# The first gate's vector on TensorE in column groups, and products of the second norm moved into the attention

## The chip, the cores and the metric

The kernel runs on one NeuronCore of a Trainium2 chip. Its engines run side by side, each through its own instruction stream in the order in which the program has it: TensorE (PE, with the weight loads PEld), VectorE (DVE), ScalarE (ACT), GpSimd (POOL), and SyncE (SP), which here issues every DMA. They meet at semaphores. The metric is the device time of one launch in microseconds; it was measured three times for the kernel before, with a median of 1086.33 us (1077.45 to 1088.35).

## The reference

One decoder layer, batch 1, 256 tokens, width 2048, everything in fp32. A conditioning vector `c` makes six vectors of 2048 numbers, which scale, shift and gate the two halves of the layer:

```
mod = silu(c) @ w_mod + b_mod                 # (2048) @ (2048, 12288)
sh1, sc1, g1, sh2, sc2, g2 = split(mod, 6)
h = rmsnorm(x, attn_norm_g) * (1 + sc1) + sh1
proj = h @ w_in                               # 2048 -> 1856
mix = concat(sliding window attention (16 heads, 2 kv heads), latent attention (8 heads))
x = x + g1 * (mix @ w_out)
h = rmsnorm(x, mlp_norm_g) * (1 + sc2) + sh2
x = x + g2 * (relu(h @ w_ff1) ** 2 @ w_ff2)   # 2048 -> 8192 -> 2048
out = rmsnorm(x, final_norm_g)
```

Each of the six vectors is a matrix-vector product with 16.8 MB of `w_mod`.

## The kernel before, in words

Activations are kept transposed: 128 features on the partitions, 256 tokens along the free axis, 16 tiles for the width. The stages follow each other.

1. **Input projection** (lines 242 to 268). For each of 16 feature tiles, `mod_col` makes one column of `sc1` and one of `sh1`, the tile is normalized, and 15 fp32 matmuls add it into eight PSUM banks with a tile `wi` of `w_in`.
2. **Attention** (lines 474 to 583). Twelve units of four heads each, eight of the windowed kind and four of the latent kind. In each step of the loop PE turns a unit's probabilities (`turn`, L376), makes the scores of the unit two steps ahead (`scores`, L405, L446, L447), three up-projections (`fill`, L509, L516) and the values (`values`, L422, L461). DVE and ACT do the softmax. All these matmuls are fp32.
3. **Output projection** (lines 608 to 629). Two halves of 16 output tiles. The weights `wo` come in, are split into a high and a low part (ACT L191, DVE L192), and three matmuls of 256 columns each (L197 to L199) are made for each pair of tiles. DVE adds `g1 * result` to `x` (L620).
4. **Second norm and first feed-forward quarter** (lines 625 to 680): the sum of squares, the reciprocal root `r2` on ACT and DVE, the 16 tiles `h2` on POOL, ACT and DVE, and the same three matmuls with `w_ff1a` (tiles `pf`).
5. **The rest of the feed-forward and the last norm**, which the change does not touch.

`mod_col(part, i)` (line 157) makes 128 numbers of one of the six vectors: a DMA of 1 MB (128 rows of the transposed `w_mod`) into a tile `wm`, and one DVE instruction (L167) that multiplies it with the broadcast vector `c_bc` and sums along 2048 elements. 96 of these make the six vectors. Part 2 is `g1`; its 16 are written before the attention, along with the first `NPRE` = 6 of the 32 products of `sc2` and `sh2` (parts 4 and 3). `pump_mod(n)` takes the next n of those 32: the output projection takes 8 in its second half (PB), the first feed-forward quarter the rest, one per tile of `kt` (LEADK), more where a tile needs them.

The written order is not the final one. A scheduler orders each engine's stream by its own estimate; the attention stands under a high priority and goes ahead of what is written before it where it can. Tiles come from rings: `wm` outside stage 1 has a ring of 2 buffers (tag `rawm`), `wi` and the other weights one of 3, the split weights `whi` and `wlo` 3 each, PSUM 8 banks. A DMA that refills a buffer waits on SP for the buffer's last reader, and all later DMAs stand behind it.

Of the kernel before, what the change touches and what calls it, by code (L numbers as in the profile page):

```python
# [9 lines left out]
F32 = mybir.dt.float32  # L10
F32R = mybir.dt.float32r
AF = mybir.ActivationFunctionType
ALU = mybir.AluOpType

P = 128
D = 2048
# [16 lines left out]
NG = 384  # L33
NPRE = 6
EVP = "A"
NORM = 'AVA'
NG1 = 0
NFILL = 3
NM = 2
NW = 3  # L40
PA = (0, 0)
PB = (0, 1)
LEAD = 0
# [6 lines left out]
LEADK = (1, 1)  # L50
PBN = 8


@with_exitstack
def kernel(
# [4 lines left out]
    vecs: bass.AP,  # L60
    w_mod: bass.AP,
    w_in: bass.AP,
    sinks: bass.AP,
# [93 lines left out]
    def mod_col(part, i):  # L157

        t = (early_ring if part < 2 else lambda n: ring("m", n))(f"wm{part}_{i}")
        nc.sync.dma_start(t, w_mod[part * KT + i])  # L160
        col = small(f"mod{part}_{i}")
# [62 lines left out]
    nc.sync.dma_start(sk_sb, sinks.broadcast_to([P, 16]))  # L224
    nsk_sb = at.tile([P, 16], F32, name="nsk_sb")
    V.tensor_scalar(out=nsk_sb, in0=sk_sb, scalar1=-1.0, scalar2=None, op0=ALU.mult)
# [57 lines left out]
    nc.sync.dma_start(con, consts)  # L284
    g1 = []
    bias_t = actp.tile([P, 16, S], F32, tag="a1", name="bias")
# [6 lines left out]
    mix = [actp.tile([P, 8, 2 * S], F32R, tag="a0", name="mix0")]  # L293
    for d in range(NG1):
        g1.append(mod_col(2, d))
    wukv = raw("wukv")
# [12 lines left out]

    for d in range(NG1, KT):  # L310
        g1.append(mod_col(2, d))
    pump_mod(NPRE)

# [159 lines left out]
    with tc.high_priority():  # L473
# [95 lines left out]
        for n, u in enumerate(units):  # L569
            if n == 8:  # L570
                mix.append(actp.tile([P, 8, 2 * S], F32R, tag="a1", name="mix1"))
            u.turn()
            if n + 2 < len(units):
                units[n + 2].scores()
            if n + 1 < len(units):
                units[n + 1].rows()
            fill(NFILL)
            u.values()


# [24 lines left out]
    for half in range(2):  # L605
# [4 lines left out]
        for dp in range(8):  # L610
            w = raw(f"wo{half}_{dp}")
            nc.sync.dma_start(w, w_out[half, dp])
            for d2 in range(2):
# [8 lines left out]
                if half:  # L622
                    ss2.add(d)
                if half == 0 or dp < PBN:
                    pump_mod((PA, PB)[half][d2])

# [173 lines left out]
def _pack(inp):  # L800
# [8 lines left out]
    def cols(a):  # L809
# [4 lines left out]
                                   cols(inp["mla_kv_norm_g"])], axis=1))  # L814
    d["w_mod"] = cc(np.asarray(inp["w_mod"])[0].T).reshape(96, P, D)
    ar = np.arange
# [23 lines left out]

_ORDER = ["xT", "cT", "vecs", "w_mod", "w_in", "sinks", "rel", "w_uq", "w_ukv", "w_out", "w_ff1a", "w_ff1b", "w_ff2",
          "consts", "onehot", "gmask"]
# [20 lines left out]
```

## Time and profile before

| | before |
|---|---|
| three runs | 1077.45, 1086.33, 1088.35 us |
| profiled execution: its own time, and its span | 1076.42 us, 1074.6 us |
| PE busy | 1025.7 us (95%), 6068 instructions |
| PE weight loads busy | 893.2 us (83%) |
| DVE busy | 744.3 us (69%), 996 instructions |
| ACT, POOL busy | 493.4 us (46%), 112.0 us (10%) |
| mean granted clock of PE | 0.985 |
| DMA | 278.21 MB, mean 259 GB/s |
| chain that ended last | PE 85%, DVE 5%, POOL 3%, DMA 3%, the rest 4% |

The span runs from the first to the last instruction; the execution's own time holds 1.8 us more. A "busy" share counts from an instruction's start to its end, and the ends of matmuls are modelled, so the pace of matmuls is better read from start to start. The trace records each fp32 matmul as two: two passes over the same columns.

### The profile page before, as it was taken

The numbers are of one execution on the slowest core, as the hardware profiler recorded it, in microseconds if no ns is written. First come the engines' busy times: TensorE is split into PE (matmuls) and PEld (weight loads), VectorE is DVE, ScalarE is ACT, GpSimd is POOL, SyncE is SP. The second block draws the span as 40 slices with busy tenths as digits, with TensorE's granted clock in tenths as the row PEclk, the third lists the DMA queues.
The fourth block names the chain that finished last, engine by engine and source line by source line (L and its number), as shares of the span: only waits on it lengthen the run. The fifth ranks groups of instructions, "written<-read, shape, count | busy, mean of one in ns | idle before, by whom it ended". The sixth has DMA issues, their size and how long they took to land.

```text
span 1074.6 us, 15326 instructions
## 1 busy us (share of the span) xinstructions
PE 1025.7 (95%) x6068; PEld 893.2 (83%) x6068; DVE 744.3 (69%) x996; ACT 493.4 (46%) x836; POOL 112.0 (10%) x88
## 2 busy tenths in 40 slices
PE   5999999999995999999999999999999999999995
PEld 4777756679995999888888888888888888888884
DVE  5777568689996789798775555556555666556564
ACT  2100076553443333784445665333666433465552
POOL 0000003000246545000000000000000000001122
PEclk9899999999998999999999999999999999999997
DMA  8999976689997765788885555555555555555542
GB/s 328 426 426 427 417 291 236 240 298 365 428 424 289 269 244 231 267 336 339 313 312 196 195 181 186 187 192 197 196 187 180 188 192 195 196 190 180 182 155 78
DMA packets 42344, 278.21 MB, mean 259 GB/s; under 512 B 4832, under 2 KB 7456, under 8 KB 11424
## 3 DMA queue, kind: packets, MB, share of 16 engines
q1 hardware_dynamic: 42272, 277.23, 68.1%
q8 instruction: 47, 0.77, 0.3%
q14 instruction: 25, 0.20, 0.1%
HBM read 275.09 MB, written 2.12 MB: 258 GB/s over the span
## 4 chain that ended last, share of the span: by engine, by line
PE 85%; DVE 5%; POOL 3%; DMA 3%; issue 2%; ACT 2%; SPq 1%; DVEq 0%; ACTq 0%; POOLq 0%
PE pd L203 22%; PE pu L203 16%; PE pd L204 11%; PE pj L268 9%; PE pu L204 9%; PE pd L198 2%; PE pd L197 2%; PE pd L199 2%; POOL xn L641 2%; DVE wm L167 2%; PE pf L199 1%; PE pf L197 1%; PE pf L198 1%; DMA wi<-in_w_in 1%; DMA wm<-in_w_mod 1%
## 5 line engine op out<-in xcount | busy, mean ns | idle before, releaser
L192 DVE TENSOR_TENSOR wf_l<-wf,wf_h 128x1024 fp32r<-128x1024 f32 x256 | 313.6, 1227 | 199.0 <-ACT wf_h L191 196.1
L191 ACT ACTIVATE wf_h<-wf 128x1024 fp32r<-128x1024 f32 x256 | 269.9, 1057 | 242.9 <-PE pd L203 177.7
L203 PE MATMUL pd<-u,wf_h 128*128 128x512 f32 x1024 | 357.0, 393 | 0.0
L204 PE MATMUL pd<-u,wf_l 128*128 128x256 f32 x1024 | 286.9, 280 | 0.0
L203 PE MATMUL pu<-h,wf_h 128*128 128x512 f32 x768 | 266.5, 391 | 0.0
L203 PEld LDWEIGHTS pd<-u,wf_h 128*128 128x128 f32 x1024 | 191.7, 187 | 43.3 <-DVE u L655 0.2
L204 PE MATMUL pu<-h,wf_l 128*128 128x256 f32 x768 | 215.1, 280 | 0.0
L204 PEld LDWEIGHTS pd<-u,wf_l 128*128 128x128 f32 x1024 | 193.5, 189 | 0.1
L203 PEld LDWEIGHTS pu<-h,wf_h 128*128 128x128 f32 x768 | 143.6, 187 | 31.4
L167 DVE CUSTOM_DVE_ANT_0 wm<-wm,c_bc,vec 128x2048 f32<-128x2048 f32 x64 | 151.7, 2370 | 1.6 <-DMA wm<-in_w_mod 1.6
L204 PEld LDWEIGHTS pu<-h,wf_l 128*128 128x128 f32 x768 | 145.2, 189 | 0.3 <-DVE wf_l L192 0.3
L268 PE MATMUL pj<-h,wi 128*128 128x256 f32 (+1 forms) x480 | 111.5, 389 | 9.6 <-ACT h L257 9.3
L268 PEld LDWEIGHTS pj<-h,wi 128*128 128x128 f32 (+1 forms) x480 | 88.1, 189 | 32.7 <-issue 11.4
L594 POOL TENSOR_TENSOR sqa<-sqa,sqr 128x256 f32<-128x256 f32 x26 | 31.8, 1222 | 717.6 <-ACT sqr L592 717.6
L167 DVE CUSTOM_DVE_ANT_0 wm<-wm,c_bc,b 128x2048 f32<-128x2048 f32 x32 | 77.3, 2414 | 28.4 <-DMA wm<-in_w_mod 28.4
L197 PE MATMUL pf<-h,wf_h 128*128 128x256 f32 x256 | 73.2, 290 | 8.6 <-ACT h L643 7.2
L199 PE MATMUL pf<-h,wf_l 128*128 128x256 f32 x256 | 72.1, 289 | 4.9 <-DVE wf_l L192 4.9
L198 PE MATMUL pf<-h,wf_h 128*128 128x256 f32 x256 | 73.1, 288 | 0.0
L197 PE MATMUL pd<-mix,wo_h 128*128 128x256 f32 x256 | 72.9, 285 | 0.0
L198 PE MATMUL pd<-mix,wo_h 128*128 128x256 f32 x256 | 72.4, 283 | 0.0
L199 PE MATMUL pd<-mix,wo_l 128*128 128x256 f32 x256 | 72.3, 283 | 0.0
L197 PEld LDWEIGHTS pf<-h,wf_h 128*128 128x128 f32 x256 | 50.2, 197 | 9.4 <-ACT h L643 7.6
(169 smaller groups left out, 1014.0 us busy)
## 6 DMA issues: line engine op xcount, KB each, us to landing
wm<-in_w_mod SPq DMA_DIRECT2D x96, 1024.0 KB, 8.1
wf<-in_w_ff SPq DMA_DIRECT2D x64, 1024.0 KB, 4.8
wf<-in_w_ff1b SPq DMA_DIRECT2D x48, 1024.0 KB, 4.8
wo<-in_w_out SPq DMA_DIRECT2D x16, 1024.0 KB, 10.1
wf<-in_w_ff1a SPq DMA_DIRECT2D x16, 1024.0 KB, 8.4
wi<-in_w_in SPq DMA_DIRECT2D x15, 928.0 KB, 12.2
x_sb<-in_xT SPq DMA_DIRECT2D x4, 512.0 KB, 6.5
bias<-g_dr SPq DMA_DIRECT2D x2, 1024.0 KB, 12.8
```

The costliest lines, as they stand in the source:

```text
L167: V.tensor_tensor_reduce(out=t, in0=t, in1=c_bc, scale=1.0, scalar=init, op0=ALU.mult, op1=ALU.add, accum_out=col)
L191: A.activation(out=hi, in_=src, func=AF.Copy)
L192: V.tensor_tensor(out=lo, in0=src, in1=hi.bitcast(F32), op=ALU.subtract)
L197: T.matmul(out, lhsT=wh, rhs=a[:, 0:S], start=start, stop=False, **kw)
L198: T.matmul(out, lhsT=wh, rhs=a[:, S : 2 * S], start=False, stop=False, **kw)
L199: T.matmul(out, lhsT=wl, rhs=a[:, 0:S], start=False, stop=stop, **kw)
L203: T.matmul(out, lhsT=wh, rhs=a, start=start, stop=False)
L204: T.matmul(out[:, 0:S], lhsT=wl, rhs=a[:, 0:S], start=False, stop=stop)
L268: T.matmul(proj(j)[: e - j * P, :], lhsT=w[:, j * P : e], rhs=h, start=(kt == 0 and j % 2 == 0), stop=(kt == KT - 1), skip_group_check=True)
L594: G.tensor_tensor(out=sqa, in0=sqa, in1=sq, op=ALU.add)
L641: G.tensor_scalar(out=xn, in0=x_sb[:, kt, :], scalar1=a2, scalar2=None, op0=ALU.mult)
```

## The change

`g1` no longer comes from DVE. `w_mod` loses its part 2, and a new input `w_g1` holds that part untransposed (2048 inputs by 2048 outputs). For each of 16 tiles of 128 inputs, `gate_steps` loads 1 MB and makes four matmuls: the stationary operand is the column `ce` of silu(c), broadcast to 32 columns, the moving one 512 outputs of `w_g1`. Matmul q writes PSUM partitions 32q to 32q+31, so the four stand in four different column groups of the array. All 64 add into one bank, `pg1`, which stays taken meanwhile. Even tiles are loaded as two halves into buffers of the rings `whi` and `wlo`, odd ones into `rawm`. `gate_out` copies the bank on ACT, turns it with four transposes, and one DVE instruction adds the bias and picks the 16 columns.

`GSTEPS` gives two tiles to each of the first eight units. `MSTEPS` gives 12 of the products of the second norm to the twelve units (6 stood there before), and `PA`, `PB` give five to each half of the output projection (0 and 8 before). So 22 instead of 14 are written ahead of the first feed-forward quarter, and 10 instead of 18 are left to it. The buffer `nsk_sb` now shares `sk_sb`.

```diff
-NPRE = 6
-NG1 = 0
-PA = (0, 0)
-PB = (0, 1)
-PBN = 8
+GSTEPS = (2, 2, 2, 2, 2, 2, 2, 2, 0, 0, 0, 0)
+MSTEPS = (0, 1, 1, 1, 1, 1, 1, 1, 2, 2, 1, 0)
+PA = (1, 3, 4, 6, 7)
+PB = (0, 1, 3, 5, 6)
...
-    for d in range(NG1, KT):
-        g1.append(mod_col(2, d))
-    pump_mod(NPRE)
+    gate = {"kt": 0, "ps": None}
+    g1_all = small("g1_all", KT)
+    g1 = [g1_all[:, d : d + 1] for d in range(KT)]
+
+    def gate_steps(n):
+        if gate["kt"] == 0:
+            gate["ps"] = bank("pg1")
+        for _ in range(n):
+            kt = gate["kt"]
+            if kt == KT:
+                return
+            if kt % 2:
+                t = ring("m", f"wg{kt}")
+                nc.sync.dma_start(t, w_g1[kt])
+                t = [t[:, 0:1024], t[:, 1024:2048]]
+            else:
+
+                t = [splp.tile([P, 1024], F32, tag=f"w{i}", name=f"wg{kt}{i}") for i in ("hi", "lo")]
+                for i in range(2):
+                    nc.sync.dma_start(t[i], w_g1[kt, :, i * 1024 : (i + 1) * 1024])
+            for q in range(4):
+                T.matmul(gate["ps"][32 * q : 32 * q + 32, :], lhsT=ce[:, kt : kt + 1].broadcast_to([P, 32]),
+                         rhs=t[q // 2][:, 512 * (q % 2) : 512 * (q % 2) + 512], start=(kt == 0),
+                         stop=(kt == KT - 1), skip_group_check=True)
+            gate["kt"] += 1
+
+    def gate_out():
+        rows = at.tile([P, 512], F32, tag="pT", name="g1_rows", bufs=4)
+        A.activation(out=rows, in_=gate["ps"], func=AF.Copy)
+        pt1 = bank("pt1")
+        for j in range(4):
+            T.transpose(out=pt1[:, j * P : (j + 1) * P], in_=rows[:, j * P : (j + 1) * P], identity=ident)
+
+        V.tensor_tensor(out=g1_all.rearrange("p (q j) -> p j q", j=4),
+                        in0=pt1.rearrange("p (j q r) -> p j q r", j=4, q=4)[:, :, :, 0],
+                        in1=vec[:, V_BMOD + 32 : V_BMOD + 48].rearrange("p (q j) -> p j q", j=4), op=ALU.add)
...
             fill(NFILL)
+            gate_steps(GSTEPS[n])
+            pump_mod(MSTEPS[n])
             u.values()
+            if n == 9:
+                gate_out()
...
-                if half == 0 or dp < PBN:
-                    pump_mod((PA, PB)[half][d2])
+                if d2 and dp in (PA, PB)[half]:
+                    pump_mod(1)
```

How it moves the streams, at three places. On PE, in the third unit of the attention (`puqn` and `pukn` are up-projections, `poa` values, `pta` transposes, `pg` the gate's bank, `wg4hi` and `wg4lo` the halves of input tile 4), before:

```order
L509 MATMUL puqn_1050<-cq_781,wuq_lo_189 128x256
L509 MATMUL puqn_1050<-cq_782,wuq_lo_191 128x256
L509 MATMUL pukn_1056<-ckv,wukv 128x256
L422 MATMUL poa_1060<-pTa_1021,vA 64x512
L376 MATMUL pta_1062<-ident,ssa_968 128x128 x4
```

and after:

```order
L540 MATMUL puqn_995<-cq_693,wuq_lo_188 128x256
L540 MATMUL puqn_995<-cq_694,wuq_lo_190 128x256
L540 MATMUL pukn_1001<-ckv,wukv 128x256
L329 MATMUL pg_858<-wg4hi,ce 32x512 x2
L453 MATMUL poa_1023<-pTa_966,vA 64x512
L329 MATMUL pg_858<-wg4lo,ce 32x512 x2
L407 MATMUL pta_1025<-ident,ssa_895 128x128 x4
```

The four matmuls of an input tile stand here as two pairs, with a matmul of the values between them.

On SP, at the end of the input projection (`wi` are the last tiles of `w_in`, `wm_15` the last products of stage 1, `con`, `bias` and `wukv` what the attention needs first), before:

```order
L160 DMA wm_15_635<-in_w_mod 128x2048
L265 DMA wi_645<-in_w_in 128x1856
L265 DMA wi_662<-in_w_in 128x1024
L265 DMA wi_662<-in_w_in 128x832
L284 DMA con<-in_consts 128x896
L289 DMA bias<-g_dr 128x8x256 x2
L297 DMA wukv<-in_w_ukv 128x2048
```

and after:

```order
L160 DMA wm_15_634<-in_w_mod 128x2048
L265 DMA wi_644<-in_w_in 128x1856
L321 DMA wg_867<-in_w_g 128x2048
L321 DMA wg_947<-in_w_g 128x2048
L265 DMA wi_661<-in_w_in 128x1024
L265 DMA wi_661<-in_w_in 128x832
L284 DMA con<-in_consts 128x896
L288 DMA bias<-g_dr 128x8x256 x2
L294 DMA wukv<-in_w_ukv 128x2048
```

Two gate tiles of 1 MB each stand ahead of the last tile of `w_in`; their buffers are those of the two products `wm_15`.

On DVE, at the second norm (`r_a`, `r_y` make the reciprocal root, `xn` and `h` the first tile, `wm` a product, `wf_l` a split weight), before:

```order
L620 SCALAR_TENSOR_TENSOR x_sb<-pd_15_2521,mod_15_754,x_sb 128x256
L179 TENSOR_SCALAR r_a<-pr_2514 128x256
L636 TENSOR_TENSOR a_0_2578<-mod_0_758,vec 128x1
L180 SCALAR_TENSOR_TENSOR r_a<-r_a,r_y 128x256
L181 TENSOR_TENSOR r_a<-r_a,r_y 128x256
L167 ISA wm_7_2706,mod_7_2708<-wm_7_2706,c_bc,vec 128x2048
L167 ISA mod_7_2708 128x1
L182 SCALAR_TENSOR_TENSOR r_y<-r_a,r_y 128x256
L192 TENSOR_TENSOR wf_l_2609<-wf_2572,wf_h_2608 128x1024
L639 SCALAR_TENSOR_TENSOR xn_0_2580<-x_sb,a_0_2578,r_y 128x256
```

and after:

```order
L655 SCALAR_TENSOR_TENSOR x_sb<-pd_15_2614,g_all,x_sb 128x256
L167 ISA wm_11_2795,mod_11_2797<-wm_11_2795,c_bc,vec 128x2048
L167 ISA mod_11_2797 128x1
L179 TENSOR_SCALAR r_a<-pr_2607 128x256
L671 TENSOR_TENSOR a_0_2667<-mod_0_955,vec 128x1
L192 TENSOR_TENSOR wf_l_2698<-wf_2661,wf_h_2697 128x1024
L180 SCALAR_TENSOR_TENSOR r_a<-r_a,r_y 128x256
L192 TENSOR_TENSOR wf_l_2739<-wf_2725,wf_h_2738 128x1024
L181 TENSOR_TENSOR r_a<-r_a,r_y 128x256
L182 SCALAR_TENSOR_TENSOR r_y<-r_a,r_y 128x256
L674 SCALAR_TENSOR_TENSOR xn_0_2669<-x_sb,a_0_2667,r_y 128x256
```

A product still stands at the norm, now ahead of the root instead of inside it, and two splits stand between the root's instructions.

## Rows read from the trace of the kernel before

**Rows 1.** By stage: window, length, busy PE, PEld, DVE, ACT, POOL; clock, DMA share, GB/s

```profile
136.70:230.00 93.30, 88.14 (x406) 58.00 (x406) 72.60 (x184) 63.21 (x195) 12.18 (x15) 1.00 0.68 252
230.00:321.50 91.50, 90.49 (x753) 90.24 (x753) 86.34 (x99) 37.70 (x46) 18.04 (x14) 1.00 0.98 398
321.50:346.00 24.50, 16.25 (x119) 15.53 (x118) 15.70 (x25) 7.99 (x13) 14.57 (x12) 0.86 0.82 315
346.00:460.00 114.00, 107.61 (x811) 103.36 (x810) 95.69 (x105) 55.09 (x89) 44.76 (x19) 0.99 0.68 253
```

**Rows 2.** Three of these stages, DVE on `wm` alone; clock, DMA share, GB/s

```profile
136.70:230.00 93.30, 36.73 (x16) 1.00 0.68 252
230.00:321.50 91.50, 36.84 (x16) 1.00 0.98 398
346.00:460.00 114.00, 41.31 (x17) 0.99 0.68 253
```

**Rows 3.** Waits of PE, 136.7 to 230 us: total, times, longest

```profile
PE pob L461 <- ACT pTb L366: 1.3, 2, 0.7
PE prq L467 <- ACT qr L366: 1.2, 2, 0.7
...
PE pvb L516 <- DVE ckv L322: 0.9, 1, 0.9
```

**Rows 4.** Waits of PE, 230 to 460 us

```profile
PE pf L197 <- ACT h L643: 7.2, 1, 7.2
PE pf L199 <- DVE wf_l L192: 4.9, 4, 3.0
PE pf L197 <- ACT wf_h L191: 1.5, 2, 0.9
```

**Rows 5.** PE's timeline: start, length, line, tiles, array rows*columns, shape, count

```profile
207.45 1.03 PE L509 MATMUL puqn<-cq,wuq_hi 128*128 128x256 f32 x4
208.31 0.59 PE L509 MATMUL puqn<-cq,wuq_lo 128*128 128x256 f32 x2
...
216.58 0.70 PE L446 MATMUL scb<-kn,qn 128*128 128x256 f32 x2
217.21 0.70 PE L447 MATMUL scb<-kra,qr 64*128 64x256 f32 x2
```

**Rows 6.** PE's timeline where two tilings of 64 rows meet

```profile
144.79 0.45 PE L562 MATMUL prk_a<-kr,seli 64*128 64x256 f32 x1 [0.65 <-ACT kr L366]
144.92 0.48 PE L405 MATMUL sca<-kA,qA 64*128 64x256 f32 x1
145.08 0.38 PE L562 MATMUL prk_a<-kr,seli 64*128 64x256 f32 x1
...
145.67 1.24 PE L405 MATMUL sca<-kA,qA 64*128 64x256 f32 x5
```

**Rows 7.** ACT's timeline: the copy of a full PSUM bank in the attention

```profile
170.99 0.60 ACT L366 ACTIVATE pTa<-pta 128x512 f32<-128x512 f32 x1 [0.43 <-PE pta L376]
```

**Rows 8.** DMA issues, 136.7 to 230 us: count, KB each, median us to landing

```profile
wm<-in_w_mod SPq DMA_DIRECT2D x15, 1024.0 KB, 4.8
```

**Rows 9.** End of the input projection: SP, DVE and PE timelines, DMA of 100:125

```profile
112.35 7.62 SPq L265 DMA_DIRECT2D wi<-in_w_in  x3
123.93 2.35 DVE L167 CUSTOM_DVE_ANT_0 wm<-wm,c_bc,vec 128x2048 f32<-128x2048 f32 x1
126.26 10.51 PE L268 MATMUL pj<-h,wi 128*128 128x256 f32 x46 [0.31 <-DMA wi<-in_w_in]
DMA packets 1573, 10.63 MB, mean 425 GB/s; under 512 B 173, under 2 KB 173, under 8 KB 780
```

**Rows 10.** DVE's timeline at the second norm

```profile
326.65 0.42 DVE L179 TENSOR_SCALAR r_a<-pr 128x256 f32<-128x256 f32 x1 [1.81 <-ACT r_y L177]
327.99 2.35 DVE L167 CUSTOM_DVE_ANT_0 wm<-wm,c_bc,vec 128x2048 f32<-128x2048 f32 x1
330.26 0.42 DVE L182 SCALAR_TENSOR_TENSOR r_y<-r_a,r_y 128x256 f32<-128x256 f32 x1
```

More of the change, by code (lines that the diff above doesn't have):

```diff
@@ L61 @@
     w_mod: bass.AP,
+    w_g1: bass.AP,
     w_in: bass.AP,
@@ L159, in mod_col @@
         t = (early_ring if part < 2 else lambda n: ring("m", n))(f"wm{part}_{i}")
-        nc.sync.dma_start(t, w_mod[part * KT + i])
+        nc.sync.dma_start(t, w_mod[(part - (part > 2)) * KT + i])
         col = small(f"mod{part}_{i}")
@@ L224 @@
     nc.sync.dma_start(sk_sb, sinks.broadcast_to([P, 16]))
-    nsk_sb = at.tile([P, 16], F32, name="nsk_sb")
+    nsk_sb = sk_sb
     V.tensor_scalar(out=nsk_sb, in0=sk_sb, scalar1=-1.0, scalar2=None, op0=ALU.mult)
@@ L284 @@
     nc.sync.dma_start(con, consts)
-    g1 = []
     bias_t = actp.tile([P, 16, S], F32, tag="a1", name="bias")
@@ L293 @@
     mix = [actp.tile([P, 8, 2 * S], F32R, tag="a0", name="mix0")]
-    for d in range(NG1):
-        g1.append(mod_col(2, d))
     wukv = raw("wukv")
@@ L308, in pump_mod @@
                 (sc2 if p == 4 else sh2)[i] = mod_col(p, i)
-    for d in range(NG1, KT):
-        g1.append(mod_col(2, d))
-    pump_mod(NPRE)
+    gate = {"kt": 0, "ps": None}
[30 more added lines that the diff above has]
+                        in1=vec[:, V_BMOD + 32 : V_BMOD + 48].rearrange("p (q j) -> p j q", j=4), op=ALU.add)
     def rmsn(chunks, gcol, n, name):
@@ L814, in _pack @@
                                    cols(inp["mla_kv_norm_g"])], axis=1))
-    d["w_mod"] = cc(np.asarray(inp["w_mod"])[0].T).reshape(96, P, D)
+    wm = np.asarray(inp["w_mod"])[0].T.reshape(96, P, D)
+    d["w_mod"] = cc(np.concatenate([wm[:32], wm[48:]]))
+    d["w_g1"] = cc(np.asarray(inp["w_mod"])[0][:, 2 * D : 3 * D]).reshape(KT, P, D)
     ar = np.arange
@@ L838, in _pack @@
     return d
-_ORDER = ["xT", "cT", "vecs", "w_mod", "w_in", "sinks", "rel", "w_uq", "w_ukv", "w_out", "w_ff1a", "w_ff1b", "w_ff2",
+_ORDER = ["xT", "cT", "vecs", "w_mod", "w_g1", "w_in", "sinks", "rel", "w_uq", "w_ukv", "w_out", "w_ff1a", "w_ff1b", "w_ff2",
           "consts", "onehot", "gmask"]
```

## The prediction, made before the changed kernel had run

> **What bounds the kernel now.** I read the busy time by stage first [rows 1]. In the attention PE is busy 88.14 of 93.30 us, at full clock, and DVE 72.60. In the output projection it is 90.49 of 91.50. So in both stages into which work is moved PE leaves 5.2 and 1.0 us, whatever DVE does. The stages that follow leave more: 24.50 less 16.25, that is 8.3 us, around the second norm, and 114.00 less 107.61, that is 6.4, in the first feed-forward quarter. Second, what DVE spends on the products `wm` [rows 2]: 16 in the attention, 36.73 us, half of its work there, so 2.3 us each. Third, what PE waits for. In the attention the long waits are for ACT, and for DVE the one row of 0.9 us [rows 3]. Behind it PE waits 7.2 us for the first `h`, and 4.9 and 1.5 us for split weights [rows 4]; in these last, DVE's stream, in which a product may stand ahead of a split, is at least partly the cause. The reader is to see that DVE is freed where PE sets the pace, and that what DVE can give back lies later and is small.
>
> **The change, part by part.**
>
> *Sixteen products leave DVE, the attention keeps some.* The 16 of part 2 (36.73 us [rows 2]) go; of the 12 written there instead eight stand ahead of the first `x_sb` in DVE's new stream. PE waited for DVE 0.9 us [rows 3], on `ckv`, where no product stands ahead. I count nothing. The cover is PE's own work; without it DVE would give back eight products.
>
> *Sixty-four matmuls come to PE.* First the pace. An fp32 matmul of 256 columns is two records; from 207.45 to 208.31 four records start, 0.215 us each [rows 5]. So 512 columns cost 0.43 a pass and 0.86 a matmul, and 64 in a row 55.0 us. Do four in different column groups run at the same time? No row of before has two column groups side by side. The nearest has two row groups: `prk_a`, `prk_b` on one 64-row half and `sca` on another. Between 144.79 and 145.67 seven records of 256 columns started [rows 6], 0.126 us each against 0.215. Both streams go at nearly full pace. I take the same for column groups, so that a set of matmuls that stand together costs what one costs, 0.86. The bounds are 0.86 a set and 0.86 a matmul.
>
> The new PE stream tells the sets. Tiles 0 and 1 and all odd tiles from 5 stand as fours: eight sets. Tile 2 is cut, its first matmul alone, the other three together with the first of tile 3, whose last three are a third set. The six even tiles from 4 are two pairs each, twelve sets. That is 23 sets, 23 x 0.86 = 19.8 us.
>
> *A change of tiling costs too.* Where the latent scores alternate between 128 and 64 rows, the next matmul starts 0.63 us later (216.58 to 217.21) where 0.43 is the pace [rows 5]: 0.20 for a change. The 23 sets make 22 places (the first two adjoin). Where a place lies between two matmuls of one kind it adds two changes, between two different kinds one; along the new stream that is 35 changes, 7.0 us. Bounds: nothing, if a column group needs no change, and 44 x 0.20 = 8.8.
>
> Here a rule speaks against the reading of rows 6. In the program both `prk` stand ahead of `sca`, yet a record of `sca` starts at 144.92, before the second of `prk_a` at 145.08 [rows 6]. The Trainium skill (TensorE: Matmul & The Clock Gate, The mechanism) says that matmuls start and end strictly in program order. The trace disagrees for row groups; what the rule would make of column groups is the second rival. The same page (Measured speedup vs the span model) gives 2.38 times for three column groups; an estimate by that is 3 x 0.86 / 2.38 = 1.08 us a set, some 5 us more in all.
>
> *The exit.* `gate_out` copies the bank on ACT, 0.60 us as a full bank of probabilities [rows 7], and four transposes of 128 columns follow, 4 x 0.11 and a change. PE's stream stands behind the copy. 1.2 us.
>
> *Waits for the gate's tiles.* A gate matmul whose tile is late stops all PE. The even tiles reuse one pair of buffers at first, so each load starts when the previous matmul is through. In the new stream about 8 us of PE's work lies between (for tile 4: values, transposes, scores, three up-projections and the matmuls of tile 3). A product of the same 1 MB lands 4.8 us after its issue [rows 8]. So mostly covered; SP's order, where a load stands behind a product's that waits for DVE, and the PSUM bank that stays taken, can make single ones late. I take 2 us, bounds 0 and 10 (two of the sixteen late by a whole landing, 2 x 4.8).
>
> *SP at the end of the input projection.* Two gate tiles now stand ahead of the last `wi`, and the second waits for the last product's end: 123.93 + 2.35 = 126.3. Before, the last three `wi` were issued between 112.35 and 119.97 [rows 9]. PE begins tile 14 at 126.26 and needs tile 15 about 6.5 us later (at 30 records of 0.215), at 132.8. Two more MB are 2.1/0.425 = 4.9 us of transfer [rows 9]; tile 14 landed at 126.3, so the first half of 15 lands near 132.4. `con`, `bias` and `wukv`, queued behind, move 5 us too, and had about that to spare. 1 us, bounds 0 and 5.
>
> *What the gate can hide in.* The wait for `qr` (1.2 us [rows 3]) now has a piece of a gate set ahead of it. -1 us, bounds 0 and -2.7 (also `ckv` and half of the rest).
>
> *The output projection* keeps about as many products as before (16 [rows 2]; now the last four of the attention's twelve slip into it, with ten of its own and two at its end), under a PE with 1.0 us to spare. Nothing.
>
> *The second norm* had a product inside its root (327.99, between `r_a` at 326.65 and `r_y` at 330.26 [rows 10]); now one stands just ahead and two splits inside. Two splits now stand where 2.35 us of a product stood: nothing. After it comes a product before the first low part of `h`. I count nothing, bounds -1 and +2.
>
> *The first feed-forward quarter* has 10 products or fewer for 17 [rows 2], none near its end. Its waits for splits are 4.9 + 1.5 [rows 4]. -4 us, bounds 0 and -6.4.
>
> **The sum.** 19.8 + 7.0 + 1.2 + 2 + 1 - 1 - 4 = +26.0 us. The profiled execution took 1076.4, so 1102.4, rounded to 1102. The median of the three runs shown is 1086.3, 10 us above that execution, one of the three stands at 1077.5; a median after may lie as far above its fast execution.
>
> **The rivals.**
>
> *The column groups run one after another.* Nothing in the trace shows column groups together, and each stream reads all 128 partitions, which the two half-height streams of rows 6 do not. Then 64 x 0.86 = 55.0 for 19.8: 1102.4 + 35.2 = 1138.
>
> *Two at a time.* If starts keep the program's order, a matmul's second pass follows its first on the same columns, and only then can the next group's first pass start beside it: a set of n costs (n + 1) x 0.43. By the sets above: 3.9 (tiles 0 and 1) + 0.9 + 2.2 + 1.7 + 12 x 1.29 + 6 x 2.15 = 37.1 for 19.8, so 1120. This is what the rule of the page on TensorE would make of it. Rows 6 speak against it.
>
> *The gate overlaps with its neighbours, and the later waits go.* If a set needs no change of tiling and a cut set goes on beside what cuts it, the streaming is 16 x 0.86 = 13.8; with the exit 1.2, -2.7 hidden and -6.4 later, +5.9: 1082, within 1%. For it: PE's queue took records out of order in rows 6. Against: each change in rows 5 costs.
>
> *Faster: DVE paces the attention.* If the busy time of PE overstates what it must do (ends are modelled), the twelve units would go by DVE's stream, 72.60 of 93.30 [rows 1]. Eight products fewer are 8 x 2.3 = 18.4 us; with 6.4 later and nothing for the gate, 1076.4 - 24.8 = 1052. It decides if PE had more than 28 us of room in the attention. Against it: PE's listed waits come to 5 us, and starts follow each other at pace in rows 5.
>
> **How the numbers follow.** My forecast (sets run together, changes cost) 0.55; two at a time 0.17; one after another 0.08; overlap and relief 0.15; DVE as the pace 0.05. Time: 1102. Within my forecast the bounds run from 19.8 + 0 + 1.2 + 0 + 0 - 2.7 - 6.4 - 1 = +10.9, 1087, to 19.8 + 8.8 + 1.2 + 10 + 5 + 0 + 0 + 2 = +46.8; all at once is unlikely, and 1088 to 1120 is its own range. The range of all, 1083 to 1128, leaves out the case of 1052, half of the overlap and the one-by-one case, 0.05 + 0.07 + 0.08. One per cent, 11 us, is about what a measurement can tell from no change here. Faster by more 0.05; within it 0.17 (overlap, and the low end of mine); slower 0.78.
>
> **What would show it.** The 64 matmuls of `pg`: the four of a set should start within some 0.1 us of each other, and a set take about 0.9 us; starts 0.43 apart mean two at a time, 0.86 apart none. The attention should last near 120 us, with DVE's `wm` there falling to some 19 us and PE at over 90%. PE's waits for DMA there should come to a few us. Waits for `wf_l` should fall. It is wrong if the attention stays within 10 us of 93, or if PE's waits, for tiles of the gate or for DVE, rather than its work make the difference.

## The result: slower by 3.5%, and the profile after

The changed kernel took 1120.26 us in the median of four runs (1119.06 to 1122.00), the kernel before beside it 1087.34 (1077.45 to 1089.67): ratio 1.035, 95% interval 1.029 to 1.041. Slower was forecast, and 1102; the range up to 1128 holds the time, but the loss is more than twice the forecast one (1.035 for 1102 / 1086.3 = 1.014). Six later executions of the changed kernel lie between 1118.26 and 1124.29.

| | after |
|---|---|
| profiled execution: its own time, and its span | 1119.06 us, 1117.3 us |
| PE busy | 1066.2 us (95%), 6200 instructions |
| PE weight loads busy | 902.0 us (81%) |
| DVE busy | 710.0 us (64%), 965 instructions |
| ACT, POOL busy | 495.9 us (44%), 89.6 us (8%) |
| mean granted clock of PE | 0.979 |
| DMA | 278.21 MB, mean 249 GB/s |

Against the profiled span of before this is 42.7 us more. Where they came is read from the first matmul of each stage. The rows of after (line, tiles, count: shortest, median, longest in ns, first to last start):

```profile
L453 PE MATMUL poa<-pTa,vA x24: 592/592/643, 159.4 to 232.9; 128*64 128x512 f32 x24
L197 PE MATMUL pd<-mix,wo_h x256: 277/283/469, 257.1 to 354.0; 128*128 128x256 f32 x128
L197 PE MATMUL pf<-h,wf_h x256: 278/283/582, 362.8 to 470.1; 128*128 128x256 f32 x128
L203 PE MATMUL pu<-h,wf_h x768: 395/398/403, 470.5 to 1012.9; 128*128 128x512 f32 x192
```

| stretch | before, us | after, us | longer by | forecast |
|---|---|---|---|---|
| up to the first gate matmul or value (L329, `poa`) | 152.7 | 157.25 | +4.6 | +1 |
| from there to the first `pd` | 75.6 | 99.85 | +24.2 | +29 |
| output projection and second norm, to the first `pf` | 105.0 | 105.7 | +0.7 | 0 |
| first feed-forward quarter (`pf`), to the first `pu` | 103.0 | 107.7 | +4.7 | -4 |
| the rest, which the change does not touch | 638.3 | 646.8 | +8.5 | 0 |

The attention's 29 are the forecast's 19.8 + 7.0 + 1.2 + 2 - 1. The stages of after in the form of [rows 1] (PE, PEld, DVE, ACT, POOL; clock, DMA share, GB/s):

```profile
159.40:257.10 97.70, 95.33 (x445) 50.60 (x441) 44.87 (x126) 48.24 (x144) 10.42 (x12) 0.98 0.70 249
257.10:354.20 97.10, 95.55 (x787) 94.59 (x787) 87.03 (x102) 37.28 (x47) 18.79 (x14) 1.00 0.96 390
354.20:362.80 8.60, 1.02 (x5) 0.41 (x3) 7.64 (x12) 3.71 (x6) 0.92 (x1) 0.80 1.02 421
362.80:470.50 107.70, 99.69 (x769) 97.88 (x770) 76.93 (x80) 42.80 (x58) 36.87 (x29) 0.94 0.59 218
```

In the attention DVE is down to 44.87 us of 97.70 and PE up to 95.33: PE sets the pace, as forecast. The waits of PE in after, from 152 to 262 us (all three rows) and from 262 to 500, answer [rows 3, 4]; the last line is one more row of [rows 3]'s view of before:

```profile
PE pvb L547 <- DVE ckv L353: 2.8, 1, 2.8
PE pob L492 <- ACT pTb L397: 1.2, 2, 0.7
PE pt L339 <- ACT g_rows L336: 1.2, 1, 1.2
...
PE pf L197 <- ACT h L678: 6.5, 1, 6.5
PE pf L199 <- DVE wf_l L192: 5.0, 5, 2.2
PE pf L197 <- ACT wf_h L191: 2.4, 1, 2.4
...
PE pf L198 <- DVE h L679: 0.5, 1, 0.5
...
PE ptb L376 <- ACT ssb L354: 1.1, 1, 1.1
```

No tile of the gate is waited for. The wait at the exit (L339) is 1.2. The waits for `qr` (1.2) and for `ssb` (1.1) that before had in the attention are gone. But `ckv` is waited for 2.8 us where it was 0.9, and the waits of the first quarter are 14.4 us where they were 13.6.

The sets of the gate, in PE's timeline of after (start, length, tiles, rows*columns, shape, count of records):

```profile
177.97 1.05 PE L329 MATMUL pg<-wg4hi,ce 128*32 128x512 f32 x4
178.95 1.07 PE L453 MATMUL poa<-pTa,vA 128*64 128x512 f32 x2
179.95 1.05 PE L329 MATMUL pg<-wg4lo,ce 128*32 128x512 f32 x4
180.94 0.66 PE L407 MATMUL pta<-ident,ssa 128*128 128x128 f32 x4
...
183.44 0.70 PE L540 MATMUL puqn<-cq,wuq_hi 128*128 128x256 f32 x2
184.07 1.06 PE L329 MATMUL pg<-wg,ce 128*32 128x512 f32 x8
185.06 1.13 PE L540 MATMUL puqn<-cq,wuq_lo 128*128 128x256 f32 x4
```

A pair (four records) holds PE for 0.98 and 0.99 us until the next start, a four (eight records) for 0.99. So they do run together, and 23 x 0.99 = 22.8. A part of the changes of tiling is in that number, a part is not. Where a set stands between two matmuls of one kind, as at 184.07 between those of `puqn`, the set starts 0.31 us behind the last record where 0.22 is their pace, and the second record behind the set comes 0.32 after the first: 0.19 more. By the prediction's own count (35 changes in 22 places) there are 13 such places, so an estimate from these rows is 22.8 + 13 x 0.19 = 25.3, where the forecast had 19.8 + 7.0 = 26.8.

### The profile page after: what moved, and what is told of

Same layout as the page of the kernel before. It is cut to its first block, busy times and chain, and to the rows that moved or that the text cites. A ratio compares the mean times of both kernels' runs of the same rounds, so it can differ in the third digit from the quotient of the medians.

```text
span 1117.3 us, 15554 instructions
## 1 busy us (share of the span) xinstructions
PE 1066.2 (95%) x6200; PEld 902.0 (81%) x6200; DVE 710.0 (64%) x965; ACT 495.9 (44%) x837; POOL 89.6 (8%) x88
## 2 busy tenths in 40 slices
DMA packets 43496, 278.21 MB, mean 249 GB/s; under 512 B 4960, under 2 KB 7584, under 8 KB 13600
## 4 chain that ended last, share of the span: by engine, by line
PE 62%; POOL 1%; DVE 1%; ACT 0%; issue 0%; DVEq 0%; POOLq 0%; ACTq 0%
PE pd L203 21%; PE pu L203 16%; PE pd L204 11%; PE pu L204 8%; PE pf L199 2%; PE pf L198 2%; PE pf L197 2%; POOL xn L676 1%; POOL xn L677 0%; ACT wf_h L191 0%; DVE x_sb L803 0%; DVE wm L167 0%; DVE wf_l L192 0%; DVEq L895 0%; PE pr L634 0%
## 5 line engine op out<-in xcount | busy, mean ns | idle before, releaser
L203 PE MATMUL pu<-h,wf_h 128*128 128x512 f32 x768 | 271.5, 399 | 0.0
L167 DVE CUSTOM_DVE_ANT_0 wm<-wm,c_bc,vec 128x2048 f32<-128x2048 f32 x48 | 115.2, 2400 | 0.4 <-DMA wm<-in_w_mod 0.4
L167 DVE CUSTOM_DVE_ANT_0 wm<-wm,c_bc,b 128x2048 f32<-128x2048 f32 x32 | 77.1, 2409 | 27.9 <-DMA wm<-in_w_mod 27.9
L197 PE MATMUL pf<-h,wf_h 128*128 128x256 f32 x256 | 74.3, 296 | 9.0 <-ACT h L678 6.5
L199 PE MATMUL pf<-h,wf_l 128*128 128x256 f32 x256 | 74.9, 293 | 5.0 <-DVE wf_l L192 5.0
L198 PE MATMUL pf<-h,wf_h 128*128 128x256 f32 x256 | 74.5, 292 | 0.5 <-DVE h L679 0.5
```

What stands on the lines that cost most here:

```text
L167: V.tensor_tensor_reduce(out=t, in0=t, in1=c_bc, scale=1.0, scalar=init, op0=ALU.mult, op1=ALU.add, accum_out=col)
L197: T.matmul(out, lhsT=wh, rhs=a[:, 0:S], start=start, stop=False, **kw)
L198: T.matmul(out, lhsT=wh, rhs=a[:, S : 2 * S], start=False, stop=False, **kw)
L199: T.matmul(out, lhsT=wl, rhs=a[:, 0:S], start=False, stop=stop, **kw)
L203: T.matmul(out, lhsT=wh, rhs=a, start=start, stop=False)
```

## The experiments

Two theories stood at first. **G**: the gate's sets on PE and a disturbed start of the attention are nearly all of it, and the +8.5 in the untouched part is a property of single executions. **S**: the products' new places cost a good part, and the pace (the time from one matmul's start to the next in a steady stretch) is a property of the program.

### The kernel before, unchanged

> The kernel before, unchanged. Of the 42.7 us between the two profiled executions 8.5 lie behind the first up-projection of the feed-forward half, where nothing was changed: its 512-column matmuls (line 203) have a mean of 391 ns before and 398 ns after at a granted clock of 1.00 in both. Theory P (the pace belongs to the execution): before's own times, 1077 beside 1086 to 1090, are these two paces, so here a profile near 1077 shows 391 ns and one near 1086 shows 398. Rival (the pace belongs to the program): 391 ns here at every time, and the spread of before's times lies elsewhere, in the attention or at the start.

Its median was 1077.81 (ten executions), the profile at 1077.50, line 203 at 391 ns. This was the quick pace, so the other was still to be seen in the kernel before. In all, 94 executions of the unchanged kernel before were timed: 53 between 1074.7 and 1080.2, 41 between 1084.3 and 1090.3, none between. Its median is drawn from two groups. No execution of the upper group of this very kernel was profiled.

### The gate alone

The products stand as before. The edit, against the changed kernel:

```diff
-MSTEPS = (0, 1, 1, 1, 1, 1, 1, 1, 2, 2, 1, 0)
-PA = (1, 3, 4, 6, 7)
-PB = (0, 1, 3, 5, 6)
+NPRE = 6
+PA = ()
+PB = (0, 1, 2, 3, 4, 5, 6, 7)
...
+    pump_mod(NPRE)
...
-            pump_mod(MSTEPS[n])
```

> One part alone: the first gate on TensorE as after, the other products placed as before (six ahead of the attention, eight in each pass of the output projection and so on). Theory G (the gate is nearly all of it): the remaining attention about 24 us longer than before's 75.6, the start of the attention some 4 us longer, the first feed-forward quarter near before's 103: +26 to +34 us on the kernel before by the medians, ratio 1.024 to 1.031. Rival S (the products' new places cost a good part, by the +4.7 us of the first quarter and the +1.4 of the output projection): then no more than +24 us here.

Median 1112.86, executions 1104.29, 1110.75, 1114.98 and 1116.13; ratio 1.030 (1.022 to 1.038). The profiled one, 1104.29, has 391 ns in the median at line 203 and is 26.8 us above the quick profile of before (1077.50). Its attention takes 98.1 us from the first `poa` to the first `pd`, after's 97.7. That speaks for G.

### The products alone

`g1` stays on DVE. The edit, against the kernel before:

```diff
-NPRE = 6
...
-PA = (0, 0)
-PB = (0, 1)
+MSTEPS = (0, 1, 1, 1, 1, 1, 1, 1, 2, 2, 1, 0)
+PA = (1, 3, 4, 6, 7)
+PB = (0, 1, 3, 5, 6)
...
-    pump_mod(NPRE)
...
+            pump_mod(MSTEPS[n])
```

> The other part alone: the first gate's sixteen products on DVE as before, the other products in the places of after. Theory G: within 1% of the kernel before, 0 to +6 us (the first feed-forward quarter may lose what it lost in after, 4.7). Rival S: +6 to +12 us. DVE gets its eight products in the attention on top of sixteen, 24 x 2.3 = 55 of its 93 us, so a wait of PE for DVE there (0.9 us before) may grow; if it grows above 5 us, that says that DVE had no room in the attention.

Both theories missed: median 1120.17, ratio 1.036 (1.029 to 1.042). The output projection takes 121.4 us from its first `pd` to its last, before's 95.5. Its window on all engines, the same on DVE's `wm` alone (two records a product), and PE's longest wait there:

```profile
229.80:351.20 121.40, 105.23 (x786) 101.95 (x786) 104.02 (x121) 36.87 (x46) 17.26 (x14) 0.92 0.90 353
```

```profile
229.80:351.20 121.40, 55.73 (x48) 0.92 0.90 353
```

```profile
PE pd L197 <- ACT wo_h L191: 14.1, 9, 6.1
```

With `g1` still on DVE, the attention has no room for the extra products: it does about as many as before, and 24 fall into the output projection. The two parts do not add (by the medians 27.9 and 35.3 for a whole of 32.9): it is the gate's move that makes room for the products. This run also takes away a premise about the first quarter: that stage has 13 products here for 16 before, and lasts 107.6 us for 103.0.

### The early gate loads held back

```diff
-        nc.sync.dma_start(t, w_uq[:, i * 1024 : min(4608, (i + 1) * 1024)])
+        uq_dma = nc.sync.dma_start(t, w_uq[:, i * 1024 : min(4608, (i + 1) * 1024)])
...
-                nc.sync.dma_start(t, w_g1[kt])
+                with tc.issue_after(uq_dma.ins):
+                    nc.sync.dma_start(t, w_g1[kt])
```

> The changed kernel with the loads of the first two odd gate tiles held until the last of the query weights has been issued, so that the input projection's last tile, the constants and the bias are not queued behind them; the order on DVE then has the root of the key norm ahead of most of unit 1's scores, nearly as before. Theory L (these two loads moved DVE's order, and with it 2.84 us of waiting for ckv and the clock of 0.60 behind it): the first values start 152.7 instead of 157.3, -4 to -5 us on the changed kernel, about 1115. Rival: the clock falls there anyway, or the held tiles now come late for their matmuls: within 1 us of the changed kernel, 1119 to 1122, with PE waits for DMA on line 329.

Theory L held at its place. Windows of after, then of this run, then the wait:

```profile
150.00:160.00 10.00, 8.17 (x24) 2.59 (x25) 4.00 (x21) 5.91 (x19) 0.00 (x0) 0.66 0.37 139
```

```profile
150.00:160.00 10.00, 9.10 (x44) 3.73 (x45) 5.18 (x25) 7.91 (x27) 1.23 (x3) 1.00 0.40 132
```

```profile
PE pvb L548 <- DVE ckv L354: 0.9, 1, 0.9
```

With the loads later, DVE again makes the root for the keys ahead of most of unit 1's scores; the wait is 0.9 again, the granted clock 1.00 for 0.66 (a mean over its two levels, 2.4 and 1.2 GHz), the first gate matmul starts at 154.7 for 157.25, and the first `pd` at 252.7 for 257.1. The gate alone, which has no gate tile ahead of the last `wi` either, waits 0.9 for `ckv` too. The whole did not gain: 1119.66 in the median. In the profiled execution, the slowest of the four (1123.98), the output projection, at 95 to 96% DMA share in both, took 104.7 us for 96.9, with 5.2 us of waits for split weights where after has 0.9; whether the other three lose there was not seen.

### One column group of a set

```diff
-            for q in range(4):
+            for q in (range(4) if kt in (0, KT - 1) else (0,) if kt % 2 else (0, 2)):
```

> The changed kernel, but of the fourteen middle gate tiles an odd one has only its first column group's matmul and an even one only one of each pair; tiles 0 and 15 keep all four. 64 matmuls become 29 while the loads, the places and the changes of tiling stay (the gate that comes out is incomplete). Theory T (column groups run together, a set costs what one matmul costs): 0 to -4 us on the changed kernel, since a set took 0.98 us there and a lone matmul 0.86. Rival (two at a time): 35 fewer at 0.43, -15 us. Rival (one after another): 35 at 0.86, -30 us.

Median 1118.37. The attention from the first `poa`, this run and then the next experiment:

```profile
158.00:252.10 94.10, 91.22 (x377) 48.89 (x377) 43.68 (x126) 48.14 (x144) 8.45 (x12) 1.00 0.71 253
```

```profile
161.00:254.20 93.20, 90.11 (x445) 49.28 (x441) 45.46 (x127) 48.51 (x144) 12.36 (x12) 0.99 0.73 264
```

35 matmuls fewer save 3.6 us on after's 97.7, where two at a time would give 15 and one after another 30. Theory T holds; the other two fall. Even the 3.6 are not the matmuls': the places did not all stay, and this stream has 20 sets for 23, so three sets of 0.99 make 3.0 of it. What a member costs is read from the sets themselves:

```profile
227.20 1.04 PE L329 MATMUL pg<-wg,ce 128*32 128x512 f32 x2
228.17 0.70 PE L540 MATMUL puqn<-cq,wuq_lo 128*128 128x256 f32 x2
```

A lone matmul (two records) holds PE for 0.97 us until the next start; over all sets here and in after the means are 0.975 for one, 0.982 for two, 0.988 for three and 0.995 for four, some 7 ns for each further member. The Trainium skill (TensorE: Matmul & The Clock Gate, Measured speedup vs the span model) gives about 4 ns for each further tile of a packed set; the rows here, with two passes for each matmul, have a little under twice that.

### Fewer sets

```diff
-            for q in range(4):
+            for q in (range(4) if kt % 2 else (2, 3, 0, 1)):
```

> The changed kernel with the two halves of each even gate tile taken in the other order (the one that lands later first), which lets the schedule put most even tiles as sets of four instead of two pairs in two places: some 17 sets instead of 23. Theory T (cost goes by sets and by changes of tiling): five to six sets of 0.98 and about ten changes of 0.2 less, -5 to -8 us at the end of the attention. Rival (cost goes by matmuls): 0. If a whole tile has to be there before its first matmul, waits for DMA on PE may take some of it back, and then they are listed on line 329.

The new PE stream has 18 sets for 23, and the attention is 93.2 us for 97.7 (window above): -4.5, 0.9 a set. That is a little short of the -5 to -8 expected, and no wait for a tile is listed. The median, 1118.49, moved by 2 to 4 us: the output projection was 98.8 us for 96.9 here.

### The changed kernel again, and before once more

> The changed kernel again, more often. Of the pace of the last 600 us two values are known, 391 ns for line 203 (before at 1076 and 1077.5; the gate alone at 1104) and 398 ns (after at 1119, the products alone at 1118, the late loads at 1124). Theory P (each execution takes one of the two, whatever the program): some executions here lie near 1109, ten below the others. Rival (the program's order decides, and the products' new places bring the slow one): all between 1117 and 1124, while before's fall into two groups.

Six executions, 1118.26 to 1124.29, none near 1109; line 203 at 398 ns. "Each execution takes one of the two, whatever the program" falls: in ten executions the changed kernel shows no second group, and both its profiles have the slow pace up to the last `pu`. Its profile at 1124.29 spent 258.4 to 357.8 us in the output projection, 2.5 more than the first one.

> The kernel before once more for its profile. Theory P: a profile at 1085 to 1088 shows a mean of 398 ns for line 203 and the stages ahead of it as in the profile at 1076; one at 1076 to 1078 shows 391. Rival: 391 at either time, and the ten us lie ahead of the first up-projection.

The profile came at 1078.96 with 391 ns, so it tells nothing new of the slower group.

### The wait at the start of the up-projection

Before's profile and after's differ in one thing where the rest of the feed-forward begins. PE's timeline, before and then after:

```profile
436.22 0.28 PE L199 MATMUL pf<-h,wf_l 128*128 128x256 f32 x1
436.34 0.39 PE L203 MATMUL pu<-h,wf_h 128*128 128x512 f32 x1
436.72 0.39 PE L204 MATMUL pu<-h,wf_l 128*128 128x256 f32 x1
436.94 0.40 PE L203 MATMUL pu<-h,wf_h 128*128 128x512 f32 x1
```

```profile
470.37 0.28 PE L199 MATMUL pf<-h,wf_l 128*128 128x256 f32 x1
470.49 0.40 PE L203 MATMUL pu<-h,wf_h 128*128 128x512 f32 x1
470.72 0.28 PE L204 MATMUL pu<-h,wf_l 128*128 128x256 f32 x1
470.84 0.40 PE L203 MATMUL pu<-h,wf_h 128*128 128x512 f32 x1
```

In before the first matmul on line 204 starts 0.38 us behind its partner, in after 0.23: there the split weights are ready in time. From there to 970 us in before and 1013 in after the pair of lines 203 and 204 takes 0.3467 us in the one and 0.3533 in the other (start to start, over 120 pairs at a time), at a granted clock of 1.00 in both. Theory **W**: the short wait brings the quick pace.

The first test takes the wait out of before, by writing the first weight's load and split ahead of the two releases (cut to the lines that move it):

```diff
+    wn = raw("wf1_2_0")
+    nc.sync.dma_start(wn, w_ff1b[0])
+    wn0 = split(wn, 0, "wf1_2_0")
     q0_out(0)
     q0_out(1)
...
-                    wh, wl = split(w, k // 8, f"wf1_{e}_{f}")
+                    wh, wl = wn0 if e == 2 and f + k == 0 else split(w, k // 8, f"wf1_{e}_{f}")
```

> The kernel before with the split of the first up-projection's first weight half written ahead of the two releases of the feed-forward accumulator, so that its low part is there when the first matmul on line 204 wants it (it came 0.15 us late in before's profile). Theory W: without a wait there the slow pace stays from the start, 398 ns, +9 to +10 us on the kernel before's 1077: 1086 to 1088 in every execution, unless a later wait sets the quick one. Rival: 391 ns and 0 us.

All ten executions at 1084.92 to 1087.81, median 1086.54; no more group at 1077, and the slow pace in the profile:

```profile
L203 PE MATMUL pu<-h,wf_h x768: 395/398/403, 438.1 to 980.5; 128*128 128x512 f32 x192
```

From the first to the last start 542.4 us, as in after (1012.9 - 470.5); before's profile has 532.4. The other way round, the wait was put into the changed kernel, into before, and into the gate alone:

```diff
+                    late = ExitStack()
+                    if e == 2 and f + k == 0:
+                        mark = small("mark", 4)
+                        late.enter_context(tc.issue_after(V.tensor_copy(out=mark, in_=pf[6][:, 0:4]).ins))
                     wh, wl = split(w, k // 8, f"wf1_{e}_{f}")
+                    late.close()
```

> The changed kernel with one dependency more: the low part of the first weight half of the up-projection (line 192) is made to follow a four-column copy that waits for the feed-forward accumulator of columns 13 of 16, so that the first matmul on line 204 waits for it once, 0.3 to 2 us. Nothing else is moved on purpose. Theory W (the last 600 us have two paces, 0.347 and 0.353 us a pair of matmuls; the quick one sets in with the first wait between a matmul of line 203 and its partner of line 204, and holds): line 203 at 391 ns, -9 us less the wait, about 1111 to 1113. Rival (the pace hangs on something else in the program or the execution): 398 ns, and 0 to +2 us on the changed kernel's 1119 to 1122.

Executions 1111.85, 1113.33, 1114.21 and 1124.70. The profiled one (1113.33) is quick:

```profile
L203 PE MATMUL pu<-h,wf_h x768: 392/395/502, 472.7 to 1007.0; 128*128 128x512 f32 x192
```

534.3 us with the waits in it. But the pace did not turn behind the waits, which end at 475. It turned here:

```profile
480.32 0.40 PE L203 MATMUL pu<-h,wf_h 128*128 128x512 f32 x1
480.56 0.40 PE L204 MATMUL pu<-h,wf_l 128*128 128x256 f32 x2
480.80 0.40 PE L203 MATMUL pu<-h,wf_h 128*128 128x512 f32 x1
```

The added dependency moved more than a wait: a wide matmul of the next output tile now stands second in PE's stream (two wide in a row at 472.70), and its narrow partner makes two narrow in a row at 480.56. So this run changes the order of the matmuls as well, and the quick pace begins where two of one width meet. It is no clean test of the wait.

> The kernel before with the same added dependency as in the changed kernel, so that the wait at the first matmul of line 204 comes in every execution and lasts longer than 0.15 us. Before's own executions come as 1075 to 1079 or as 1084 to 1088. Theory W: every execution at 1076 to 1080 and none above 1083, line 203 at 391 ns. Rival: the two groups stay, some executions at 1085 or more.

A miss: eight executions at 1078.19 to 1082.84, four at 1087.49 to 1090.37.

> The first gate on TensorE, the other products as before, and the added dependency. The gate alone gave 1104.3 in its profile, where the quick pace set in at 500.85 us behind a wait of 0.35, and 1111 to 1116 in its other executions. Theory W: all executions near 1103 to 1106, the quick pace from the first up-projection on; on the kernel before at its quick pace +26 to +29 us, the forecast's 26 for the change. Rival: the same spread as without the dependency.

A miss too: 1103.24, 1112.31, 1116.09 and 1116.57, and the profile, with a wait of 0.44 us at that place, keeps the slow pace. That expectation also misread the gate alone: there the pace turned at about 494 us, ahead of the wait at 500. So no wait at that place went with the slow pace each time, but a wait does not set the quick one reliably.

Behind the last `pu` every profile of this order has one more place with two wide and then two narrow matmuls in a row, and the pace can turn there in either direction. In before it goes from the quick to the slow at 975 us (0.3533 from there), in after from the slow to the quick at 1019 (0.3467), in the changed kernel's second profile it stays slow. So of the +8.5 in the rest, +10.0 lie between the first `pu` and the last, and -1.5 behind it.

### The same matmuls in another order

```diff
     def mm2(out, wh, wl, a, start, stop):
-        T.matmul(out, lhsT=wh, rhs=a, start=start, stop=False)
-        T.matmul(out[:, 0:S], lhsT=wl, rhs=a[:, 0:S], start=False, stop=stop)
+        late_mm.append((wh, wl, a, start, stop))
+        if len(late_mm) == 2:
+            for h, _, b, s0, _ in late_mm:
+                T.matmul(out, lhsT=h, rhs=b, start=s0, stop=False)
+            for _, l, b, _, s1 in late_mm:
+                T.matmul(out[:, 0:S], lhsT=l, rhs=b[:, 0:S], start=False, stop=s1)
+            late_mm.clear()
```

This form makes wide, wide, narrow, narrow of two k, the second wide, narrow, narrow, wide.

> The kernel before with the same matmuls of the last 600 us in another order: the wide ones of two k first, then the two narrow ones. Theory A (the two paces belong to the alternation wide, narrow): one pace in every execution; if it is the quick one's 0.3467 us for a wide and a narrow matmul, all near 1077, if the overhead is less, below that; no second group. Rival: two groups 9 to 10 us apart stay, at whatever level.

> The kernel before with the order wide, narrow, narrow, wide for each two k. Theory A: one pace in every execution, and no groups 9 to 10 us apart. Rival: the groups stay.

The groups are gone. Pairs: ten executions from 1076.18 to 1081.72, median 1079.89. Swapped: 1077.17 to 1080.65, median 1078.45. The kernel before beside them had both groups (1076.73 to 1088.96, median 1085.61); the ratios are 0.996 (0.993 to 0.998) and 0.995 (0.992 to 0.998). Against the kernel before beside them that is under half a per cent; the quick group of before alone (1076.73 to 1080.17) is as fast as either form. What the other orders take away is the slow group.

> The changed kernel with the wide matmuls of two k first, then the narrow ones. If this order has one pace, the difference from the kernel before in the same order is the price of the change without the pace: by the stages of the profiles +4.6 at the start of the attention, +24.2 in it, +1.4 in the output projection, -0.6 in the norm, +4.7 in the first quarter, together +34 us; by the forecast +26. At the quick pace that is about 1110.

> The changed kernel in the order wide, narrow, narrow, wide. The same as for the pairs: about +34 us on the kernel before in that order by the stages, +26 by the forecast; about 1110 if the pace is the quick one.

Medians 1112.40 (1110.03 to 1114.18) and 1112.01 (1111.57 to 1113.50). The pairs in before and in the changed kernel:

```profile
L208 PE MATMUL pu<-h,wf_h x768: 390/396/400, 437.9 to 972.5; 128*128 128x512 f32 x192
```

```profile
L208 PE MATMUL pu<-h,wf_h x768: 393/396/398, 471.0 to 1005.6; 128*128 128x512 f32 x192
```

534.6 us in both, so now the untouched part costs both kernels the same (639.7 and 639.6 us from the first `pu` to the end). The change costs 1112.40 - 1079.89 = 32.5 us in the one order, 1112.01 - 1078.45 = 33.6 in the other.

## Why the prediction was right in direction and wrong in size

**Column groups run together: right.** 0.99 us a set by rows. The sum for both, 26.8, was some 1.5 too high against the 25.3 estimated from the rows: beside 0.86 a set the changes come to 5.5 for 7.0 (0.13 inside each of 23 sets, 0.19 outside 13 of them).

**Exit 1.2, waits for tiles 2 (0 to 10), hidden 1 (0 to 2.7):** the wait at the exit alone is 1.2, and the four transposes behind it take 0.5 more. No wait for a tile came. 2.3 were hidden, the waits for `qr` and `ssb`. The attention as a whole: +24.2 for +29, and 25.3 + 1.7 - 2.3 = 24.7 accounts for it. "Near 120 us": 93.3 + 24.2 = 117.5. DVE's `wm` at 19 there: after has 18.05 from the first `poa` to the first `pd`:

```profile
159.40:257.10 97.70, 18.05 (x15) 0.98 0.70 249
```

**SP at the end of the input projection, +1 (0 to 5): right queue, wrong victim.** `wi` did not come late in the first profile of after (in the second PE waited 1.4 us for it). The two early loads changed the order on DVE, `ckv` came 2 us later, and the clock fell behind it: +4.6. With the loads held the wait for `ckv` is back at 0.9 and the first gate matmul 2.5 us earlier.

**Output projection and second norm:** +0.7 where 0 was forecast, inside the bounds.

**First feed-forward quarter, -4 (0 to -6.4): the step that failed.** It read the waits for `wf_l` and `wf_h` [rows 4] as a debt of DVE's products. Products and length by profile: before 16 and 103.0 us, the gate alone 17 and 105.3, after 13 to 14 (the prediction counted 10) and 107.7, the products alone 13 and 107.6. Fewer products did not shorten it, and PE's waits there come to 13.6 us in before, 12.8 in the gate alone and 14.4 in after.

The clock is not the reason either. It is 0.97 in before and 0.94 in after, but the changed kernel's second profile, the late loads and the changed kernel in pairs last the same 107.6 us at 0.95, and the gate alone with the wait lasts 105.7 at 0.93. What differs is when the split weights come. 27 us behind the first `pf` PE had started 168 of the stage's 768 records in before, and 144 in after and in the gate alone; 40.5 us behind it, 266 and 218 in before and after. On ACT the high part of a weight (`wf_h`) stands behind tiles `h` that wait for POOL's `xn`. The first split after the start of the stage has two such `h` right ahead of it in before and four in after (the last of them shown), and starts 7.3 and 10.2 us behind the first `pf`, at 333.27 and 362.85:

```profile
340.15 0.51 ACT L643 ACTIVATE h<-xn,mod 128x256 fp32r<-128x256 f32 x1 [1.21 <-POOL xn L642]
340.57 1.05 ACT L191 ACTIVATE wf_h<-wf 128x1024 fp32r<-128x1024 f32 x1
```

```profile
370.88 0.51 ACT L678 ACTIVATE h<-xn,mod 128x256 fp32r<-128x256 f32 x1 [1.22 <-POOL xn L677]
372.61 0.51 ACT L678 ACTIVATE h<-xn,mod 128x256 fp32r<-128x256 f32 x1 [1.22 <-POOL xn L677]
373.02 1.05 ACT L191 ACTIVATE wf_h<-wf 128x1024 fp32r<-128x1024 f32 x1
```

That ACT's new order makes the whole of the 4.7 is argued from these rows; no run put the order back.

**The untouched rest, 0, and the base of the sum: the other step that failed.** The rest is not in the sum at all, and its miss, 8.5, is as large as the quarter's 8.7. It is +8.5 in the profile, without a wait or a clock to show for it. The prediction put its 26 on the profiled execution, 1076.4, noted that the median lies 10 us above it, and left that gap out of the 1102. The runs say that it is the two paces: before's executions come in two groups 10 us apart, the kernel before with the wait removed is in the upper group every time and has the slow pace in its profile, and the two other orders have no second group. On the median, 1086.3, the same 26 would have given 1112.

The relief that the step on the first quarter looked for did come at one place, the first matmul on line 204, and there its effect ran the other way: without the wait the slow pace came in all ten executions of before with the wait removed, and after's ten lie where it puts them. Since before takes the quick pace in 53 executions of 94, the change costs 33 us at one pace, 33 by the first medians (where before's lay in the upper group), and 42.7 from profile to profile.

At one pace the account closes by stages: 26 forecast, +3.6 at the start, -4.8 in the attention, +0.7 and +8.7 in the first quarter make 34.2, against 32.5 and 33.6 measured.

**The rivals.** One after another and two at a time are out by the rows of the sets and by the run with one group. Overlap with relief is out by the price of a set. DVE as the pace is out: DVE's busy time in the attention fell by 28 us between [rows 1] and after, and the attention grew.

**Open:** what decides between the two paces. That the strict alternation of the two widths is a condition is shown by the two other orders; why a wait turns it in some executions, and why it turned at 494 us without one, is not. Nor is it shown that ACT's order alone lengthens the first quarter.

## What to carry to other kernels

A set of small matmuls in different column groups costs PE nearly the same with one, two or four members (0.975, 0.982 and 0.995 us here), so what counts is how many sets the order makes; bring all members of a set together before placing it. Work moved to the engine that sets the pace is paid in full there, and the relief of another engine is worth only the waits that it is shown to cause: fewer products beside an equal wait means that something else made the wait, so follow the wait back through each engine's stream first. When times of one kernel form two groups, find the stretch that differs by start-to-start pace before forecasting, since a profile belongs to one of the groups and a change can choose the group. An edit that is to add one wait can also reorder a scheduled stream, so compare the order of the records before reading the result.

## What the runs showed of the hardware that was not expected

An alternation of 128x512 and 128x256 matmuls in this precision ran at either 0.3467 or 0.3533 us a pair, for hundreds of microseconds, at a granted clock of 1.00 in both, with no wait listed. It makes 10 us over the 1536 pairs (768 of the up-projection, as many of the down-projection among them) from the first `pu` to the last. Two wide and then two narrow, or wide, narrow, narrow, wide, ran at one pace, close to the quick one: 534.6 us from the first `pu` to the last against 532.4 and 542.4.

The Trainium skill (TensorE: Matmul & The Clock Gate, Back-to-back issue gap) lists 518 and 262 cycles for these widths, as the gap of isolated matmuls; an estimate by that page is 0.325 us a pair at 2.4 GHz. The trace has 0.347 and 0.353 with a weight load to each matmul: the measurement decides.
